# RWKV-7 / HGRN2 block on one core: the last head outputs read back through dead state tiles, masks and bounds built ahead of x, and a planner reserve of 0.8 in place of 0.45

## The chip, the cores and the metric

The kernel runs on one core of one Trainium2 chip. The metric is the device time of one execution in microseconds (us). The engines are named as the profile names them: PE is the matrix engine (PEld its weight loads), DVE the vector engine, ACT the scalar engine, POOL the GpSimd engine, SP the engine whose queue issues the DMAs. Each of them takes its instructions strictly in the order in which they were written, and waits at one whose input isn't there.

## The reference

One residual block on 512 tokens of 1024 channels, in float32:

```python
xn = rmsnorm(h, attn_pre_norm)
z = xn @ w_in                                  # 1024 -> 4096 + 3328 + 2048 columns
o_a = hgrn2_chunkwise(q, log(f), 1 - f, v)     # 8 heads of 128, chunks of 32
y = rwkv7_scan(r, w, k, v, -kk, kk * a)        # 16 heads of 64, state 64 x 64
merged = sigmoid(ga) * (o_a' @ w_branch_a) + sigmoid(gb) * (o_b @ w_branch_b)
h = h + rmsnorm(merged @ w_out, attn_post_norm)
h = h + rmsnorm(conv_ffn(rmsnorm(h, ffn_pre_norm)), ffn_post_norm)
```

`o_b` is made from `y` by a norm per head, a bonus term and the gate `g`.

## The kernel before

**Products in three passes.** Every large product is made of a high and a low part in fp32r: hi·hi, hi·lo and lo·hi. For each block of 128 columns a raw weight tile of 128x1024 is loaded from HBM (`raw`, two buffers in the pool `wraw`), ACT casts it (`whi_t`), POOL or DVE subtracts (`wlo_t`), and PE runs 24 matmuls of 128x512 into a PSUM bank (`zps`). The product that gives the HGRN values runs 256 wide (`vps`).

**Stage 0 (lines 483 to 651), written out by hand.** It loads x, multiplies the unnormalised x (`xuh`, `xul`) by the first five blocks of `w_in` and divides by the row norm afterwards (`rbs`, the results lie in the tile `ini`), so that PE needn't wait for the norm. Then it makes the normalised x (`xr`, cast to `xh`, rest in `xl`, eight pieces) that all later blocks use, and the first two weight tiles of the HGRN value product (`vn0`, `vn1`). `masks()` and `more_masks()` build the triangular masks of the chunks, `consts()` and `more_consts()` the lower bounds of the HGRN gate (`fa`, `fb`, `nfb`). In the kernel before, `more_masks()` and `more_consts()` are DVE's last work of the stage.

**Stage 1 (up to `plan.run()`), ordered by a planner.** The token mixers are written as generators that yield one instruction at a time: `lora_in`, `front`, `solve` and `chain` for RWKV (eight pairs of heads), `hgrn` for HGRN, `load`, `splits`, `gemm` and `evac` for the weights and the products. The class `Plan` gives each candidate a time at which its inputs would be ready (ends of earlier instructions by a cost table, plus a hop between engines), takes the earliest, and writes it out. `MARGIN` is added to the ready time of every PE instruction whose input or bank comes from another engine, so that it is placed later among PE's other matmuls. `AT0` gives the times at which DVE, ACT and POOL start, counted from PE. The plan is only an order: nothing on the chip waits for its times.

`chain(hb)` is the serial part: eight chunks, in each three PE steps (`us`, `yp` banks) with DVE between them. After its last chunk it makes the head norm (`ys`, `ym`, `yss`), transposes (`yt`), multiplies by the gate (`gps`) and stores to `ob_d`. The last pair of heads stays in SBUF instead.

`ob_in()`, spawned when the last chain ends, loads the other seven outputs back from `ob_d` and splits them into `oh1` and `ol1` (`oh`, `ol` in the profile). The three products `B1` with `w_branch_b` that end the stage need all eight. Before, it uses the `raw` tiles of the weights, and holds the counter `live["raw"]`, for which `load()` waits too.

**Stage 2** is the rest: the branch products (`yps`), `w_out` (`mix`), and the FFN (`zps` and `dn` by lines 354 to 356). The diff doesn't touch it.

In the trace the helper at line 237 or 387 records nearly all instructions of stages 1 and 0, so that tiles, not lines, tell them apart.

Of the kernel before, what the change touches and what calls it, by code (L numbers as in the profile page):

```python
# [16 lines left out]
P = 128  # L17
# [25 lines left out]
NWIN = 66  # L43
NX = 2
RAWS = 1
MARGIN = 0.45
AT0 = (4, 3, 1)
XG = ((0, 0),)
MORD = ((0, 0), (1, 0), (2, 0), (3, 0), (0, 1), (1, 1), (2, 1), (3, 1))
WOT = (7.0, 9.2, 13.5, 15.0)  # L50
# [28 lines left out]
class Plan:  # L79
# [76 lines left out]
    def cost(self, op):  # L156
        out = op.outs[0]
        n = out.free_size()
        scalars = sum(a.free_size() == 1 for a in op.ins) if n > 1 else 0
        far = any(a.space == PSUM for a in op.ins + op.outs)  # L160
        if op.key == "T":
            n, m = op.args[2].free_size() if op.name == "matmul" else n, op.args[1].free_size()
            if op.args[1].dtype == F32R:
                op.us = n / 2400 + (0.0165 if n > 256 else 0.013)
                if op.args[1].shape[0] < P:
                    op.us *= 1.86
            elif op.name == "transpose":
                op.us = 0.109 if n == 128 else 0.055
            elif n == 64 and m == 64:
                op.us = 0.111 if out.offset < 64 * out.ap[0][0] else 0.0535  # L170
            elif n == 64 and m == 128:
                op.us = 0.195
            elif n == 128 and op.args[1].shape[0] == 64:
                op.us = 0.118
            elif n == 32:
                op.us = 0.044 if m == 32 else 0.155
            else:
                op.us = max(0.218, n / 600)
            op.form = tuple(32 if x <= 32 else 64 if x <= 64 else P for x in (op.args[1].shape[0], m))
        elif op.key == "V":  # L180
            if op.name == "tensor_reduce":
                n = op.ins[0].free_size()
            rate = 160 if op.name == "reciprocal" else 960
            if op.name in ("tensor_copy", "tensor_scalar", "tensor_single_scalar") and not far:
                rate = 1920
            op.us = 0.069 + n / rate + 0.061 * scalars
            if op.name == "tensor_tensor_scan":
                op.us = 0.069 + n / 480
            if n == 64 and out.shape[0] == 64 and far:
                op.us += 0.07  # L190
            op.shared = not far and op.name in ("tensor_copy", "tensor_scalar", "tensor_single_scalar", "tensor_tensor",
                                                "scalar_tensor_tensor", "tensor_tensor_scan")
        elif op.key == "A":
            op.us = (0.051 if far else 0.093) + n / 1200 + (0.093 if scalars or len(op.outs) > 1 else 0.0)
            if far and n == 256 and out.shape[0] < P:
                op.us += 0.11
            elif n <= 64:
                op.us += 0.1
        elif op.key == "G":
            op.us = 0.147 + n / (470 if op.name == "tensor_tensor" else 840)  # L200
            if op.kw.get("op") == ALU.pow:
                op.us = 0.3 + n * 0.165
        else:
            op.us = 0.475
# [70 lines left out]
def block_kernel(ctx: ExitStack, tc: tile.TileContext, out: bass.AP, xT: bass.AP, xN: bass.AP,  # L275
# [22 lines left out]
    def rsq(t, n, eps, seq=lambda op: op):  # L298
        seq(G.tensor_single_scalar(t, t, eps, op=ALU.add))
        seq(G.tensor_tensor(t, t, mhalf[:, 0:n], op=ALU.pow))  # L300
# [28 lines left out]
    def split_unit(src, hi=None, lo=None, eng=None):  # L329
        raw = wraw.tile([P, 1024], F32, name="raw", tag="raw")  # L330
        nc.sync.dma_start(raw, src)
        if hi is None:
            hi, lo = ring_tiles()
        eng = eng or G
        for key, op in zip(("hi", eng), split(hi, lo, raw, eng)):
            if key in wlast:
                after(op, wlast[key])
            wlast[key] = op
        return hi, lo
# [7 lines left out]
    def seq(key, op):  # L347
        if key in last:
            after(op, last[key])
        last[key] = op  # L350
        return op
# [147 lines left out]
    with tc.tile_pool(name="init", bufs=1) as ip, tc.tile_pool(name="pinit", bufs=1, space=PSUM) as pi:  # L499
# [103 lines left out]
        for k in range(KD):  # L603
            init_mm(2, k)
            if k == KS:
                for t in range(NT):
                    Ti.matmul(sps[:, t : t + 1], acc[0][:, t * P : t * P + P], ones[:, 0:1], start=True, stop=True)
        Vi.tensor_single_scalar(ss, sps, 1.0 / D, op=ALU.mult)
        rsq(ss, NT, EPS, lambda op: seq("Gi", op))
        dg = ip.tile([P, NT, P], F32, name="dg")  # L610
        for t in range(NT):
            Ai.activation(dg[:, t], ident, AF.Identity, scale=ss[:, t : t + 1])
        init_w(B_V, V, "Vi")
        Ai.activation(le, le, AF.Exp)
        masks()
        for k in range(KD):
            init_mm(3, k)
            if k == KR:
                for t in range(NT):
                    Ti.matmul(rb[:, t * P : (t + 1) * P], ones, dg[:, t], start=True, stop=True)  # L620
        vn0 = split_unit(whi[0, 0], None, None, V)
        seq("Ai", wlast["hi"])
        seq("Vi", wlast[V])
        Ai.copy(rbs, rb)
        Ai.copy(zs0[2], zps[2])
        for k in range(KD):
# [2 lines left out]
        for k in range(KD + 1):  # L629
            if k < KD:  # L630
                xrs[k] = ip.tile([P, S], F32, name="xr", tag="xr", bufs=6)
                Vi.scalar_tensor_tensor(xrs[k], xt[:, k], pc("g_pre", k), rbs, op0=ALU.mult, op1=ALU.mult)
                Ai.copy(xh[:, k], xrs[k])
            if k >= 1:
                j = k - 1
                Vi.tensor_tensor(xl[:, j], xrs[j], xh[:, j].bitcast(F32), op=ALU.subtract)
        Vi.tensor_tensor(zs0[0], zs0[0], rbs, op=ALU.mult)
        Vi.tensor_tensor(zs0[2], zs0[2], rbs, op=ALU.mult)
        Vi.tensor_tensor(zs0[3], zps[3], rbs, op=ALU.mult)
        vn1 = (wspl.tile([P, 1024], F32R, name="whi_t", tag="hi"), wspl.tile([P, 1024], F32R, name="wlo_t", tag="lo"))  # L640
        init_wh(None, vn1, whi[0, 1])
        wturn[0] += 1
        rawf = wraw.tile([P, 1024], F32, name="raw", tag="raw")
        nc.sync.dma_start(lwr0, wlg[0, :, 0 : 2 * P])
        nc.sync.dma_start(rawf, win[B_F])
        Vi.tensor_tensor(zs0[4], zps[4], rbs, op=ALU.mult)
        Vi.tensor_tensor(zs0[1], zs0[1], rbs, op=ALU.mult)
        more_masks()
        more_consts()
        hi_pri.__exit__(None, None, None)  # L650

    cin.close()
# [350 lines left out]
    def ob_in():  # L1003
        for k in range(0, HB - 1, 2):
            n = min(2, HB - 1 - k)
            yield done(("post", k + n - 1))
            yield lambda: live["raw"] < 2
            live["raw"] += 1
            raw = wraw.tile([P, 1024], F32, name="raw", tag="raw")
            rv = raw.rearrange("p (k s) -> p k s", k=2)[:, 0:n]  # L1010
            yield D1.dma_start(rv, ob_d[k : k + n].rearrange("k p s -> p k s"))
            hi, lo = (o[:, k : k + n] for o in osb)
            yield A1.copy(hi, rv)
            yield V1.tensor_tensor(lo, rv, hi.bitcast(F32), op=ALU.subtract)
            live["raw"] -= 1
            for i in range(n):
                fin.add(("obin", k + i))

# [594 lines left out]
```

## Time and profile before

| | us |
|---|---|
| median of 3 runs | 1237.76 (1235.39 to 1238.46) |
| the profiled execution, whole | 1233.13 |
| its span in the trace | 1231.4 |
| PE busy | 1174.2 (95%) |
| DVE busy | 718.1 (58%) |
| POOL busy | 546.8 (44%) |
| ACT busy | 523.1 (42%) |

A row of the timeline gives the start, the length, the engine, the line, what is written from what, the shape, the count, and in brackets how long the engine stood idle before it and what ended that. The row of a window gives its length, and for PE, PEld, DVE, ACT and POOL the busy time and the number of instructions, then the clock that PE was granted (1.00 is full), the share of the DMA engines and GB/s. A row of waits gives the total, the number and the longest.

### The profile page before, as it was taken

The numbers are of one execution on the slowest core, as the hardware profiler recorded it, in microseconds if no ns is written. First come the engines' busy times: TensorE is split into PE (matmuls) and PEld (weight loads), VectorE is DVE, ScalarE is ACT, GpSimd is POOL, SyncE is SP. The second block draws the span as 40 slices with busy tenths as digits, with TensorE's granted clock in tenths as the row PEclk, the third lists the DMA queues.
The fourth block names the chain that finished last, engine by engine and source line by source line (L and its number), as shares of the span: only waits on it lengthen the run. The fifth ranks groups of instructions, "written<-read, shape, count | busy, mean of one in ns | idle before, by whom it ended". The sixth has DMA issues, their size and how long they took to land. (4 is left out here: it accounts for less than half of the span.)

```text
span 1231.4 us, 19053 instructions
## 1 busy us (share of the span) xinstructions
PE 1174.2 (95%) x7140; PEld 964.4 (78%) x7140; DVE 718.1 (58%) x1607; ACT 523.1 (42%) x1010; POOL 546.8 (44%) x572
## 2 busy tenths in 40 slices
PE   8789999999999999989999699999999999999997
PEld 7667778878787888767888587887988888888786
DVE  5899788797798776876673535336432323222213
ACT  6534544545464454433454333226443433433321
POOL 2154344342545243433344445423465755756521
PEclk9899999998999999999999799999999999999999
DMA  5122311212232222222323357364433322324232
GB/s 180 52 73 61 87 59 48 79 39 80 62 87 76 87 77 68 71 82 60 90 63 101 113 166 271 103 205 137 127 97 95 110 86 86 103 75 121 83 116 86
DMA packets 57244, 118.83 MB, mean 96 GB/s; under 512 B 21952, under 2 KB 25152, under 8 KB 57152
## 3 DMA queue, kind: packets, MB, share of 16 engines
q1 hardware_dynamic: 57152, 117.62, 31.2%
q8 instruction: 56, 0.92, 0.3%
q14 instruction: 36, 0.29, 0.1%
HBM read 104.22 MB, written 13.37 MB: 95 GB/s over the span
## 5 line engine op out<-in xcount | busy, mean ns | idle before, releaser
L237 POOL TENSOR_TENSOR wlo_t<-raw,whi_t 128x256 fp32r<-128x256 f32 x280 | 227.0, 840 | 298.4 <-ACT whi_t L237 283.9
L312 POOL TENSOR_TENSOR wlo_t<-raw,whi_t 128x1024 fp32r<-128x1024 f32 x75 | 182.9, 2446 | 85.9 <-ACT whi_t L312 85.8
L237 PE MATMUL zps<-xh,wlo_t 128*128 128x512 f32 x488 | 202.5, 415 | 0.0
L237 PE MATMUL zps<-xh,whi_t 128*128 128x512 f32 x488 | 201.5, 413 | 0.0
L237 PE MATMUL zps<-xl,whi_t 128*128 128x512 f32 x488 | 201.1, 412 | 0.0
L312 ACT CAST whi_t<-raw 128x1024 fp32r<-128x1024 f32 x77 | 80.1, 1048 | 159.8 <-DMA raw<-wup 65.9
L1474 DVE SCALAR_TENSOR_TENSOR u<-zps,pr,u 128x511 f32<-128x511 f32 x40 | 30.0, 750 | 187.7 <-ACT u L1473 186.9
L237 ACT CAST whi_t<-raw 128x1024 fp32r<-128x1024 f32 x74 | 77.4, 1046 | 123.8 <-PE zps L237 55.6
L354 PE MATMUL zps<-x2h,whi_t 128*128 128x512 f32 x320 | 124.7, 390 | 0.0
L356 PE MATMUL zps<-x2h,wlo_t 128*128 128x512 f32 x320 | 124.7, 390 | 0.0
L355 PE MATMUL zps<-x2l,whi_t 128*128 128x512 f32 x320 | 124.5, 389 | 0.0
L237 PEld LDWEIGHTS zps<-xh,whi_t 128*128 128x128 f32 x488 | 93.7, 192 | 17.1 <-issue 0.7
L237 PEld LDWEIGHTS zps<-xh,wlo_t 128*128 128x128 f32 x488 | 93.9, 192 | 16.7 <-issue 0.7
L237 PEld LDWEIGHTS zps<-xl,whi_t 128*128 128x128 f32 x488 | 93.5, 192 | 17.2 <-issue 0.7
L356 PEld LDWEIGHTS zps<-x2h,wlo_t 128*128 128x128 f32 x320 | 60.1, 188 | 12.7
L354 PEld LDWEIGHTS zps<-x2h,whi_t 128*128 128x128 f32 x320 | 60.1, 188 | 12.6
L355 PEld LDWEIGHTS zps<-x2l,whi_t 128*128 128x128 f32 x320 | 60.1, 188 | 12.5
L1499 POOL TENSOR_TENSOR th<-th,u 128x512 f32<-128x512 f32 x22 | 28.4, 1291 | 72.4 <-DVE u L1475 72.4
L1473 ACT ACTIVATE u<-zps,pr 128x512 f32<-128x512 f32 x40 | 31.0, 775 | 39.4 <-PE zps L356 39.4
L237 PEld LDWEIGHTS us<-sv,X 128*128 128x128 f32 x256 | 37.6, 192 | 6.9 <-DVE sv L237 2.9
L237 PEld LDWEIGHTS yp<-sv,X 128*128 128x128 f32 x256 | 37.9, 192 | 6.1 <-DVE sv L237 1.3
L355 PE MATMUL yps<-ol,whi_t 128*128 128x512 f32 x104 | 40.9, 394 | 1.7 <-DVE ol L312 1.7
(392 smaller groups left out, 2661.6 us busy)
## 6 DMA issues: line engine op xcount, KB each, us to landing
raw<-win SPq DMA_DIRECT2D x64, 512.0 KB, 3.7
raw<-wup SPq DMA_DIRECT2D x44, 512.0 KB, 3.6
raw<-wdn SPq DMA_DIRECT2D x22, 512.0 KB, 3.6
raw<-wbr SPq DMA_DIRECT2D x16, 512.0 KB, 3.9
raw<-whi SPq DMA_DIRECT2D x8, 512.0 KB, 3.7
sg_d<-sg SPq DMA_DIRECT2D x16, 256.0 KB, 2.1
gate<-sg_d SPq DMA_DIRECT2D x8, 512.0 KB, 5.6
raw<-wout SPq DMA_DIRECT2D x8, 512.0 KB, 3.5
```

The costliest lines, as they stand in the source:

```text
L237: op.ins_ = self.seq(op.key, op.fn(*op.args, **op.kw))
L312: return A.copy(hi, raw), eng.tensor_tensor(lo, raw, hi.bitcast(F32), op=ALU.subtract)
L354: T.matmul(o, lh, rh, start=start, stop=False)
L355: T.matmul(o, lh, rl, start=False, stop=False)
L356: T.matmul(o, ll, rh, start=False, stop=stop)
L1473: A.activation(u, ps, AF.Identity, scale=pc("cw2", b), bias=pc("cb", b))
L1474: V.scalar_tensor_tensor(u[:, 1:S], ps[:, 0 : S - 1], pc("cw1", b), u[:, 1:S], op0=ALU.mult, op1=ALU.add)
L1499: G.tensor_tensor(th, th, uv_, op=ALU.mult)
```

## The change

Four things: `MARGIN` from 0.45 to 0.8; `AT0` from (4, 3, 1) to (5.5, 2.5, 0.0), with one more shape (128 elements from PSUM, under 128 partitions) that is costed 0.11 dearer on ACT; stage 0 in another order; and `ob_in()` through two new tiles of the names `sv` and `bk` instead of `raw`. `sv` holds the chain's state and `bk` the front's keys; their pool has one buffer for each name, so that a new tile of the name takes the place of the old one when that is dead. Both have the size of a raw tile.

```diff
-MARGIN = 0.45
-AT0 = (4, 3, 1)
+MARGIN = 0.8
+AT0 = (5.5, 2.5, 0.0)
...
-            if far and n == 256 and out.shape[0] < P:
+            if far and n in (128, 256) and out.shape[0] < P:
...
+        Ai.activation(le, le, AF.Exp)
+        masks()
         Vi.tensor_single_scalar(ss, sps, 1.0 / D, op=ALU.mult)
+        more_consts()
+        more_masks()
         rsq(ss, NT, EPS, lambda op: seq("Gi", op))
...
         init_w(B_V, V, "Vi")
-        Ai.activation(le, le, AF.Exp)
-        masks()
...
-        vn0 = split_unit(whi[0, 0], None, None, V)
-        seq("Ai", wlast["hi"])
-        seq("Vi", wlast[V])
         Ai.copy(rbs, rb)
...
+            if k == 2:
+                vn0 = split_unit(whi[0, 0], None, None, V)
+                seq("Ai", wlast["hi"])
+                seq("Vi", wlast[V])
...
-        Vi.tensor_tensor(zs0[3], zps[3], rbs, op=ALU.mult)
         vn1 = (wspl.tile([P, 1024], F32R, name="whi_t", tag="hi"), wspl.tile([P, 1024], F32R, name="wlo_t", tag="lo"))
...
+        Vi.tensor_tensor(zs0[3], zps[3], rbs, op=ALU.mult)
         Vi.tensor_tensor(zs0[4], zps[4], rbs, op=ALU.mult)
         Vi.tensor_tensor(zs0[1], zs0[1], rbs, op=ALU.mult)
-        more_masks()
-        more_consts()
...
-            yield lambda: live["raw"] < 2
-            live["raw"] += 1
-            raw = wraw.tile([P, 1024], F32, name="raw", tag="raw")
-            rv = raw.rearrange("p (k s) -> p k s", k=2)[:, 0:n]
+            raw = mx.tile([P, NCH, 2, 64], F32, name="sv" if k % 4 else "bk")
+            rv = raw.rearrange("p (k n) h c -> p k (n h c)", k=2)[:, 0:n]
...
-            live["raw"] -= 1
```

The order of the instructions shows what these do. The first place is the end of stage 0 on DVE; in this piece of the difference, rows with a minus stood there before and rows with a plus stand there now. `ini` are the normalised first products, `wlo_t` is the low part of `vn1`, and the rows that leave are masks and bounds.

```order
+L387 TENSOR_TENSOR wlo_t<-raw,whi_t 128x1024
 L387 TENSOR_TENSOR ini<-zps_176,ini 128x512
-L387 TENSOR_TENSOR wlo_t<-raw,whi_t 128x1024
 L387 TENSOR_TENSOR ini<-zps_177,ini 128x512
 L387 TENSOR_TENSOR ini<-ini 128x512
-L387 TENSOR_TENSOR strict<-incl,ident 64x64 x2
-L387 COPY mo<-strict 128x64 x2
-L387 TENSOR_TENSOR mf<-mf,bm_146 128x64
-L387 TENSOR_TENSOR mf<-mf,strict 128x64
-L387 TENSOR_SCALAR mf<-mf 128x64
-L387 TENSOR_TENSOR lsum<-le 128x8
-L387 RECIPROCAL lsum<-lsum 128x8
```

The thirteen small instructions (four more rows of them follow) now stand right behind `ss`, before the first `xr`; the low part of `vn0` has moved the other way, from ahead of the eight `xr` to behind the third.

The second place is ACT behind the last chunk of the last chain. Before, these rows stand there; `oh` is the split of the read-back, `hf`, `p`, `hq`, `hg` belong to HGRN's last head, `lgh` to the gate:

```order
L237 CAST oh_7164<-raw 128x1024
L237 ACTIVATE ys<-ys 128x512
L237 ACTIVATE p_7191<-hf,fa,fb 128x16x16 x2
L237 CAST oh_7164<-raw 128x1024
L237 CAST lgh<-lgr 128x128
L237 CAST oh_7164<-raw 128x1024
L237 ACTIVATE hq<-zps 128x512
L237 CAST whi_t<-raw 128x1024
L237 CAST oh_7164<-raw 128x512
L237 COPY ys<-yt 64x4x64 x4
L237 ACTIVATE hg<-zps 128x512
L237 CAST whi_t<-raw 128x1024
```

And these now (`on` is HGRN's last norm, `sg` a sigmoid gate that is stored):

```order
L237 ACTIVATE ys<-ys 128x512
L237 CAST oh_7345<-bk 128x1024
L237 CAST lgh<-lgr 128x128
L237 CAST whi_t<-raw 128x1024
L237 ACTIVATE sg<-zps 128x512
L237 CAST oh_7345<-sv 128x1024
L237 ACTIVATE on,hss<-ops 128x128 x3
L237 COPY ys<-yt 64x4x64 x4
L237 CAST oh_7345<-bk 128x1024
L237 ACTIVATE on,hss<-ops 128x128
L237 CAST oh_7345<-sv 128x512
L237 CAST whi_t<-raw 128x1024
```

HGRN's last head is nearly through by now, the head norm's square stands ahead of the first `oh`, and only two `oh` stand ahead of the copies from `yt` (four before).

The third place is on PE, in the middle of stage 1, where the scores of one HGRN head (`hsc`) meet a chain and a front. So it stood before in head 2:

```order
L237 MATMUL hsc<-qi,kj 64x64
L237 MATMUL hsc<-qi,kj 32x32 x4
L237 MATMUL us<-sv,X_1840 128x64 x2
L237 MATMUL aps<-zwah,lw 128x512
L237 MATMUL aps<-zas,lw 128x512
L237 MATMUL hsc<-qi,kj 32x32 x2
L237 MATMUL yp<-sv,X_1840 128x64 x2
L237 MATMUL hsc<-qi,kj 64x64
```

And now, in a later head:

```order
L237 MATMUL us<-sv,X_4374 128x64 x2
L237 MATMUL hsc<-qi,kj 32x32 x5
L237 MATMUL hsc<-qi,kj 64x64
L237 MATMUL hsc<-qi,kj 32x32 x6
L237 MATMUL hsc<-qi,kj 64x64
L237 MATMUL hsc<-qi,kj 32x32
L237 MATMUL nps<-blk_102,sq 128x2
L237 MATMUL yp<-zs,qd_517 128x64
```

In both, no 512-wide matmul of a weight block (`zps`) stands between the small ones. Before, the 28 small groups of a head's scores stand so, with rows of a chain and a front among them, in one head; now in three, in one of them with rows of `solve` and a single `zps` row as well.

## The prediction

> **What bounds the kernel now.** I read the page first, then windows over the three stages, then PE's waits and what ended them.
>
> ```profile
> span 1231.4 us, 19053 instructions
> PE 1174.2 (95%) x7140; PEld 964.4 (78%) x7140; DVE 718.1 (58%) x1607; ACT 523.1 (42%) x1010; POOL 546.8 (44%) x572
> PEclk9899999998999999999999799999999999999999
> 100.00:650.00 550.00, 530.47 (x4070) 434.31 (x4069) 433.58 (x1162) 263.25 (x614) 229.68 (x314) 0.99 0.24 71
> 640.34 0.40 PE L237 MATMUL zps<-xl,whi_t 128*128 128x512 f32 x1
> 640.57 0.40 PE L237 MATMUL zps<-xh,wlo_t 128*128 128x512 f32 x1
> ```
>
> PE is busy for 1174.2 of 1231.4 us, and it is the bound in every stage; its busy time is made of a fixed list of matmuls, of which the wide ones follow each other every 0.23 us (640.34 to 640.57). The change takes no matmul away. It can only win what PE loses: 57.2 us of idle time, and stretches in which the granted clock is below full (the 7 and the 8s of PEclk). The middle, 100 to 650, holds 19.5 us of the idle time; the rest sits in few places, and the change is aimed at two of them.
>
> **The start.** Stage 0 ends in a wait.
>
> ```profile
> 28.60 1.23 DVE L312 TENSOR_TENSOR wlo_t<-raw,whi_t 128x1024 fp32r<-128x1024 f32 x1 [3.75 <-ACT whi_t L312]
> 33.34 1.41 DVE L387 SCALAR_TENSOR_TENSOR xr<-xt,pr,ini 128x512 f32<-128x512 f32 x2
> 46.82 0.39 PE L237 MATMUL vps<-wlo_t,xh 128*128 128x256 f32 x1 [1.32 <-DVE wlo_t L387]
> 47.88 0.45 DVE L387 TENSOR_TENSOR strict<-incl,ident 64x64 f32<-64x64 f32 x2
> 50.10 0.17 DVE L387 TENSOR_SCALAR nfb<-fb 128x8 f32<-128x8 f32 x1
> 50.19 0.72 ACT L237 ACTIVATE zwa<-ini,cm 128x512 f32<-128x512 f32 x1 [6.13 <-DVE fb L387]
> 53.08 0.60 ACT L237 CAST zwah<-zwa 128x512 fp32r<-128x512 f32 x1
> 53.79 0.55 PE L237 MATMUL wps<-zwah,lw 64*128 64x512 f32 x1 [4.79 <-ACT zwah L237]
> 52.00:56.00 4.00, 2.01 (x5) 1.35 (x6) 2.54 (x4) 3.91 (x7) 1.18 (x2) 0.75 0.00 0
> 56.00:60.00 4.00, 4.00 (x18) 3.34 (x16) 3.64 (x6) 3.49 (x6) 0.90 (x1) 0.50 0.02 4
> ```
>
> PE waits 1.32 for the low part of `vn1`, then 4.79 for `zwah`; `zwah` waits for `zwa`, and `zwa` stood 6.13 behind DVE's last bounds. The masks and bounds (47.88 to 50.27) take 2.4 us of DVE there. Now they stand behind `ss`, in the 3.75 us in which DVE waits for ACT ahead of 28.60, so they cost nothing while they fit: 2.4 into 3.75, and their masks are copied by ACT while it would wait for the norm. If they don't, the whole x preparation slips by the excess. With ACT's copies and the `vn0` split out of the way, the first `xr` can follow the split that ends at 29.83, say at 29.9 where it was 33.34: 3.4 earlier, less the 1.2 of the `vn0` split that now stands inside: 2.2. `zwa` comes 2.2 + 2.4 = 4.6 earlier, of which I keep 4.1; a weight cast that the planner now puts ahead of `zwah` takes about 1 back. So `zwah` is ready at about 50.6 instead of 53.7. PE, without the 1.32, would be at `wps` at 47.7, and the new order puts 15 half-width matmuls more ahead of it, 15 times half of 0.23, or 1.7: 49.4. What is late next is `zwah` by 1.1 us. The two waits shrink from 6.1 to 1.1: **−5.0**. Bounds: −6.1 if `zwa` needs only its own input, −3 if it still hangs on the last `ini`.
>
> Behind the wait the clock was 0.75 for 2.01 busy us and 0.50 for 4.00: 0.5 + 2.0 = 2.5 us lost. With an idle time of 1.1 this goes: **−2.5** (0 if a short wait drops it too).
>
> **The front of the first head.**
>
> ```profile
> 76.16 0.37 PE L237 MATMUL scb<-X,bk 64*128 64x128 f32 x1 [1.22 <-DVE bk L237]
> 82.57 0.46 PE L237 MATMUL sc<-X,bk 64*128 64x128 f32 x2 [2.74 <-DVE X L237]
> 93.44 0.66 PE L237 MATMUL tp<-ident,bk 128*128 128x128 f32 x4 [1.21 <-DVE bo L237]
> ```
>
> 5.2 us, all behind DVE. The new order has 66 wide matmuls instead of 49 between `nps` and `sc`, but DVE now has the eight reciprocals ahead of `bk`, and between `bps` and `tp` the 16 wide matmuls have become the scores and one wide one. The second wait goes, the third grows: **−1** (−4 to +2).
>
> **The end of stage 1.** This is the largest single place.
>
> ```profile
> 668.01 0.55 PE L237 MATMUL yp<-sv,X 128*128 128x64 f32 x4
> 669.16 0.69 DVE L237 TENSOR_TENSOR ys<-ys 128x512 f32<-128x512 f32 x1 [1.80 <-ACT ys L237]
> 676.57 1.67 POOL L237 TENSOR_TENSOR yss<-yss,mhalf 128x8 f32<-128x8 f32 x1
> 681.00 10.26 SPq L237 DMA_DIRECT2D raw<-ob_d  x2
> 684.40 1.04 ACT L237 CAST oh<-raw 128x1024 fp32r<-128x1024 f32 x1 [4.49 <-DMA raw<-ob_d]
> 685.97 0.69 DVE L237 SCALAR_TENSOR_TENSOR hq<-hq,zps 128x512 f32<-128x512 f32 x1 [3.54 <-ACT hq L237]
> 687.41 1.09 PE L237 MATMUL yt<-ident,ys 128*128 128x128 f32 x4 [8.10 <-DVE ys L237]
> 693.67 0.62 ACT L237 CAST oh<-raw 128x512 fp32r<-128x512 f32 x1 [6.80 <-DMA raw<-ob_d]
> 695.74 0.80 PE L237 MATMUL gps<-zgzh,lgh 128*128 128x512 f32 x1 [2.65 <-ACT ys L237]
> 680.00:700.00 20.00, 9.94 (x28) 7.77 (x29) 10.96 (x15) 6.45 (x11) 7.91 (x9) 0.66 0.30 96
> raw<-ob_d SPq DMA_DIRECT2D x3, 512.0 KB, 3.6
> 746.04 0.50 PE L355 MATMUL yps<-ol,whi_t 128*128 128x512 f32 x1 [1.69 <-DVE ol L312]
> ```
>
> The read-back needs `raw` buffers that the weights hold, so its DMAs stand in SP's queue (10.26 us for two), ACT stands at `oh`, DVE at `hq` behind ACT, and the norm that PE's `yt` needs stands behind `hq` although POOL had its part at 678.2. PE idles 8.10 and then 2.65, and its clock is 0.66 over these 20 us: 9.94 busy us lose 9.94 × 0.34 = 3.4.
>
> Now `bk` is dead since the last front and `sv` at the last chain matmul, so the first two DMAs issue behind `lgr` at once, and the weight loads no longer queue with them. I count from the last `yp`. The norm: from `ys` at 669.16 on, six steps of about 0.7 on DVE and ACT bring it to 4.4 by my estimate, and POOL's two (the second 1.67) to 7.3. DVE's own queue: the first read-back issues at about 0.9, lands 3.6 later, cast 1.04, subtraction 1.2 (a split of that size at 28.60), two small HGRN steps, then the scaled `ys` 0.7: about 8.6. PE's rows up to `yt` are now 29 wide matmuls and ten small HGRN ones, 39 × 0.23 = 9.0 (before, 47 wide ones, 10.8; the trace has 687.41 less 8.10 less 668.56, 10.7). So the wait goes, with 0.4 to spare, and what is late next is again the read-back: each us that a load needs beyond 4 is a us at `yt`. `gps` stands 14 wide matmuls, 3.2 us, behind `yt`, and the copies between them no longer wait for two read-backs: no wait. I keep 0.4 of risk: **−10.3** and **−3.4** for the clock. Bound: a load that shares the engines takes 5.5 rather than 3.6, which gives 1.5 back, and no clock is lost. The reuse makes ACT and DVE free `bk` before the third load: behind it in SP's queue stands a weight for `B1`, which starts some 20 us after the chain; that is the cover. HGRN's last head now ends ahead of `B1` instead of inside it, so the 1.69 at 746.04 goes as well: **−1.7**.
>
> **The middle, where the reserve works.**
>
> ```profile
> PE fps L237 <- DVE Tn L237: 5.4, 6, 2.2
> PE dps L237 <- DVE Tn L237: 4.4, 4, 1.5
> PE yt L237 <- DVE ys L237: 3.9, 4, 2.0
> ```
>
> These and five smaller groups, all on DVE too, make up the 19.5 us of idle time between 100 and 650, in some 20 waits of about 1 us. `MARGIN` places each waiting step 0.35 us, or one and a half wide matmuls, later per hop, and behind two hops 0.7. Taking 0.35 off each of 20 waits gives 7, taking 0.7 off gives 12 or so, since the small ones end at zero: **−7** (−14 to +2, because a faster PE also leaves DVE, busy for 433.6 of 550, less time). The price of the reserve is latency: between two steps of a chain stand seven wide matmuls, before six. It shows nowhere while such matmuls are left, and 69 still stand behind the last chain (before 129).
>
> The clock is the other side.
>
> ```profile
> 287.67 0.76 PE L237 MATMUL us<-sv,X 128*128 128x64 f32 x4 [0.30 <-DVE sv L237]
> 294.21 0.80 PE L237 MATMUL zps<-xh,wlo_t 128*128 128x512 f32 x1
> 292.00:296.00 4.00, 4.00 (x28) 3.47 (x27) 3.52 (x19) 2.44 (x6) 0.00 (x0) 0.62 0.00 0
> 296.00:300.00 4.00, 4.00 (x13) 3.38 (x13) 2.33 (x7) 1.63 (x3) 1.13 (x2) 0.53 0.00 0
> 540.00:548.00 8.00, 7.61 (x75) 6.13 (x76) 1.59 (x11) 2.04 (x4) 0.92 (x2) 0.79 0.35 82
> 560.00:568.00 8.00, 6.84 (x87) 6.16 (x87) 2.70 (x7) 3.26 (x9) 1.38 (x5) 0.79 0.23 68
> ```
>
> At 292 to 300 the clock falls to about 0.6 although PE waited at most 0.30: ahead of 294.21 stand some 7 us of small matmuls only, scores among chain steps. It costs 4 × 0.38 + 4 × 0.47 = 3.4 us. At 540 and 560 it costs 7.61 × 0.21 + 6.84 × 0.21 = 3.0 more, behind waits. In the new order three heads have such a bunch, by my estimate 4 to 6 us long. Three falls would cost 10.2, two 6.8; I take 8.4, against 6.4 now: **+2** (−6 to +8).
>
> A rule bears on this. The Trainium skill, "TensorE: Matmul & The Clock Gate", Part 1, says that PE falls to half clock after an idle window of about 3.4 us and needs about as long a busy one to come back. The fall behind 4.79 us agrees; that at 292 does not, and the measurement decides.
>
> **The sum.** −5.0 − 2.5 − 1 − 10.3 − 3.4 − 1.7 − 7 + 2 = −28.9. The profiled execution took 1233.13 (span and 1.7 around it), so its like would take 1204.2. It was faster than the three timed runs; against their median, 1237.8 − 28.9 = **1208.9**.
>
> **The rivals.**
>
> The middle gives nothing: DVE's lag grows with PE's speed, the 19.5 us stay, and three to four bunches cost the clock, +4 instead of +2. −28.9 + 7 + 2 gives 1218 (to 1222 with a fourth). For it speaks that every wait quoted there ends at DVE, which the change makes no faster.
>
> The bunches cost nothing: only waits of several us drop the clock. Then the middle's term is −6.4 instead of +2: 1200.5. Against it speaks 292 to 300. It is what the rule of the Trainium skill named above would make of the new order.
>
> The read-back is late again, behind `lgr` and a `sg` store in SP's queue, so that ACT stands at `oh` as before and the end gives nothing: −28.9 + 13.7 gives 1222.6. Against it: the loads now come before the weights.
>
> It is slower: the longer chain. One wide matmul more in each of 24 steps is 24 × 0.23 = 5.5 us a head, 44 us over eight. This is free as long as matmuls are left behind the last chain; 69 × 0.23 = 16 us are. Should DVE's lag push the chains by more than that, PE would idle through the rest: 44 − 28.9 gives 1253. It decides from the point at which the wait ahead of `B1` passes 29 us.
>
> The change doesn't do what it says: fitted to the planner's own times, it moves the waits to other hops, and only part of the start's 5 us stays: about 1234 to 1239, no difference. That is within 0.3% (3.7 us), about what a measurement of this kernel can tell.
>
> **How the numbers follow.** Forecast 55%, middle nothing 18%, bunches free 9%, read-back late 7%, no difference 5%, slower 6%. The forecast's own range, from the terms' bounds taken together and not all at one end, is 1200 to 1217. To 1198 below and 1226 above lie the forecast and the next three, with some of each lost at the ends: about 8 in 10. Faster than 0.3%: 0.55 + 0.18 + 0.09 + 0.07 = 0.89; same 0.05; slower 0.06.
>
> **What would show it.** Right: `zwa` at about 46 and no wait over 1.5 us at `wps`; clock 1.0 at 56 to 60; `yt` of the last head without a wait, `oh` waiting under 1.5 us, SP's read-backs under 2 us each; PE's waits on `fps`, `dps` and `yt` in the middle halved; two or three falls of the clock behind bunched scores. Wrong: a new wait of several us at `yps` or `B1`, waits in the middle of 19.5 us or more, or falls of the clock in more than four places.

## The result and the profile after

| | before | after |
|---|---|---|
| median, us | 1236.58 (4 runs, 1234.72 to 1238.46) | 1197.4 (4 runs, 1196.47 to 1199.69) |
| profiled execution, us | 1233.13 | 1197.6 |
| its span, us | 1231.4 | 1195.9 |
| PE idle in the span, us | 57.2 | 25.1 |

The ratio is 0.9686, 95% interval 0.9664 to 0.9708: clearly faster, by 39.2 us between the medians and by 35.5 between the profiled executions. Forecast were 28.9 less and 1208.9 us; the time lies 2.6 us under the forecast's own range (1200 to 1217) and 0.6 under the wide one (1198 to 1226).

First the page of the changed kernel.

```profile
span 1195.9 us, 19056 instructions
PE 1170.8 (98%) x7140; PEld 961.8 (80%) x7140; DVE 722.5 (60%) x1607; ACT 523.2 (44%) x1010; POOL 544.7 (46%) x572
PEclk9999999999999999999999999999999999999999
```

PE does the same 7140 matmuls, now in 98% of the span, and none of the forty slices has a clock under nine tenths. Where the time went shows in its windows (columns as before: length, busy time of PE and of the others, then the clock).

```profile
52.00:56.00 4.00, 3.91 (x22) 3.15 (x23) 3.51 (x7) 3.97 (x7) 0.00 (x0) 1.00 0.33 121
56.00:60.00 4.00, 3.92 (x22) 3.09 (x21) 2.19 (x7) 3.97 (x7) 3.26 (x4) 1.00 0.00 0
100.00:650.00 550.00, 542.57 (x4125) 444.52 (x4126) 438.72 (x1182) 269.54 (x627) 232.97 (x323) 0.99 0.26 75
660.00:680.00 20.00, 19.63 (x101) 16.00 (x101) 15.09 (x24) 13.04 (x28) 13.64 (x15) 1.00 0.47 155
```

The two windows behind the start, 0.75 and 0.50 before, have their full clock. The middle idles 7.4 us (550 less 542.57) where it idled 19.5. The 20 us in which the last head's `yt` and `gps` stand idle 0.4 at full clock; before, these two stood in 680 to 700, which idled 10.1 at 0.66.

The start, by the timeline:

```profile
25.63 0.46 DVE L387 TENSOR_TENSOR strict<-incl,ident 64x64 f32<-64x64 f32 x2
28.48 1.23 DVE L312 TENSOR_TENSOR wlo_t<-raw,whi_t 128x1024 fp32r<-128x1024 f32 x1 [1.43 <-ACT whi_t L312]
29.67 1.42 DVE L387 SCALAR_TENSOR_TENSOR xr<-xt,pr,ini 128x512 f32<-128x512 f32 x2
34.10 1.23 DVE L312 TENSOR_TENSOR wlo_t<-raw,whi_t 128x1024 fp32r<-128x1024 f32 x1 [1.64 <-ACT whi_t L312]
43.75 0.73 ACT L237 ACTIVATE zwa<-ini,cm 128x512 f32<-128x512 f32 x1 [0.50 <-DVE ini L387]
48.35 0.63 ACT L237 ACTIVATE zwa<-zwa 64x512 f32<-64x512 f32 x1 [2.01 <-DVE zwa L237]
50.13 0.60 ACT L237 CAST zwah<-zwa 128x512 fp32r<-128x512 f32 x1
50.83 0.47 PE L237 MATMUL wps<-zwah,lw 64*128 64x512 f32 x1 [1.43 <-POOL wlo_t L237]
52.09 0.47 PE L237 MATMUL wps<-zws,lw 128*128 128x512 f32 x1 [0.37 <-ACT zws L237]
```

The masks run inside DVE's wait for ACT: that wait has shrunk from 3.75 to 1.43, and the split behind it starts at 28.48 (28.60 before). The first `xr` follows at 29.67. The low part of `vn0` (34.10) brings a wait of 1.64 for ACT, so that DVE's last `xl` ends only 0.8 earlier than before. `zwa` starts at 43.75 instead of 50.19, but its second step (48.35) waits 2.01 for DVE, which has the last splits and `ini` ahead of it; `zwah` starts at 50.13 instead of 53.08. The wait at `wps` is 1.43. The row names POOL's `wlo_t`, which ends at the same time; what `wps` reads is `zwah`, and that ends at 50.73, 0.1 ahead of the matmul, so I put the wait down to `zwah`.

The front of the first head, in PE's timeline:

```profile
75.91 0.37 PE L237 MATMUL scb<-X,bk 64*128 64x128 f32 x1 [0.77 <-DVE bk L237]
80.22 0.46 PE L237 MATMUL sc<-X,bk 64*128 64x128 f32 x2 [0.63 <-DVE X L237]
90.13 0.66 PE L237 MATMUL tp<-ident,bk 128*128 128x128 f32 x4 [0.24 <-DVE bo L237]
```

5.2 us of waits have become 1.6; the third, which I expected to grow, is the smallest.

The end of stage 1, and the first branch product behind it. First two more rows of SP's queue before (the prediction shows that of 681.00):

```profile
668.49 6.89 SPq L237 DMA_DIRECT2D raw<-ob_d  x2
690.93 0.33 SPq L237 DMA_DIRECT2D raw<-ob_d  x1
```

And the changed kernel:

```profile
661.99 0.55 PE L237 MATMUL yp<-sv,X 128*128 128x64 f32 x4
663.53 0.40 SPq L237 DMA_DIRECT2D bk<-ob_d  x1
663.98 0.46 SPq L237 DMA_DIRECT2D sv<-ob_d  x1
667.54 1.05 ACT L237 CAST oh<-bk 128x1024 fp32r<-128x1024 f32 x1 [0.51 <-DMA bk<-ob_d]
668.17 1.67 POOL L237 TENSOR_TENSOR yss<-yss,mhalf 128x8 f32<-128x8 f32 x1
670.69 0.38 SPq L237 DMA_DIRECT2D bk<-ob_d  x1
671.07 1.21 DVE L237 TENSOR_TENSOR ys<-ys,yss 128x512 f32<-128x512 f32 x1
671.17 0.45 SPq L237 DMA_DIRECT2D raw<-wbr  x1
672.34 0.66 PE L237 MATMUL yt<-ident,ys 128*128 128x128 f32 x4
673.98 0.33 SPq L237 DMA_DIRECT2D sv<-ob_d  x1
674.74 1.05 ACT L237 CAST oh<-bk 128x1024 fp32r<-128x1024 f32 x1 [0.20 <-DMA bk<-ob_d]
710.50 0.50 PE L355 MATMUL yps<-ol,whi_t 128*128 128x512 f32 x1 [0.98 <-DVE ol L312]
```

A single issue of a read-back takes 0.33 to 0.46 in SP's queue, before as now; the 6.89 and 10.26 of the rows of before reach from one issue to the end of the next. What has changed is when the four come: counted from the end of the last `yp`, at −0.1, 6.4, 12.4 and 22.4 us before, and now at 1.0, 1.4, 8.2 and 11.4. ACT waits 0.51, 0, 0.20 and 0.54 at the four `oh` (0.47, 3.15, 4.49 and 6.80 before), and `yt` and `gps` have no wait. The cover at `yt`, the work that PE has until its input comes, is just enough: the scaled `ys` ends at 672.28, `yt` starts at 672.34. Of 1.69 at `yps` 0.98 is left.

What is left of the waits in the middle, in PE's waits from 100 to 650 (total, times, longest):

```profile
PE fps L237 <- DVE Tn L237: 2.9, 2, 1.5
PE yt L237 <- DVE ys L237: 1.4, 2, 1.1
PE yp L237 <- DVE zs L237: 1.0, 2, 0.8
```

**The clock, cell by cell.** Narrow windows laid over each trace show that a fall goes to exactly half clock and lasts 3.4 us or a whole multiple of it, and that the falls of one execution lie on one grid of 3.41 us. I call a stretch of that grid a cell, and count fallen cells. The kernel before has ten between 30 us and the end of the FFN; the changed kernel has three, at 123, 509 and 823 us. Here is the one at 509, with a cell on each side.

```profile
505.47:508.88 3.41, 3.41 (x58) 2.94 (x46) 2.57 (x10) 2.75 (x7) 0.00 (x0) 1.00 0.00 0
508.88:512.29 3.41, 3.41 (x21) 2.94 (x21) 2.61 (x12) 1.34 (x4) 0.00 (x0) 0.50 0.53 84
512.29:515.71 3.42, 3.42 (x20) 2.88 (x20) 1.67 (x6) 2.91 (x7) 1.74 (x3) 1.00 0.30 115
594.22:597.63 3.41, 3.41 (x65) 2.95 (x66) 1.56 (x4) 0.86 (x3) 0.00 (x0) 1.00 0.02 5
```

The first row is a cell inside a bunch of scores without a `zps` row (505.0 to 509.3 by the timeline), PE busy all through; the next cell has 0.50. The bunch at 592.4 to 597.4 is longer, its cell (last row) has as many small matmuls, and no fall follows. Of the six bunches of 4 to 6 us in this kernel (stretches of stage 1 without a matmul 256 or 512 wide of a weight block) one dropped the clock.

### The profile page after: what moved, and what is told of

The parts are those of the page before. It is cut to its first block, busy times and chain, and to the rows that moved or that the text cites. A ratio compares the mean times of both kernels' runs of the same rounds, so it can differ in the third digit from the quotient of the medians.

```text
span 1195.9 us, 19056 instructions
## 1 busy us (share of the span) xinstructions
PE 1170.8 (98%) x7140; PEld 961.8 (80%) x7140; DVE 722.5 (60%) x1607; ACT 523.2 (44%) x1010; POOL 544.7 (46%) x572
## 5 line engine op out<-in xcount | busy, mean ns | idle before, releaser
L237 PE MATMUL zps<-xl,whi_t 128*128 128x512 f32 x488 | 198.4, 407 | 0.0
L237 ACT COPY ys<-us 64x128 f32<-64x128 f32 x64 | 16.7, 261 | 62.4 <-DVE sv L237 47.1
```

The lines of the kernel that those rows point to most:

```text
L237: op.ins_ = self.seq(op.key, op.fn(*op.args, **op.kw))
```

## The experiments

Theory A, after the result: the terms of the prediction are the right places, each worth what the waits and the clock of its place show. Its rivals: the worth of a part hangs on the others (the reserve above all), and what the clock loses isn't set by how long a bunch is. All times are medians, all ratios are to the kernel before on the same chip. PE idle and fallen cells come from one profiled execution each.

**The parts alone, on the kernel before.** The read-back:

```diff
-            raw = wraw.tile([P, 1024], F32, name="raw", tag="raw")
+            raw = mx.tile([P, NCH, 2, 64], F32, name="sv" if k % 4 else "bk")
```

> The kernel before with the read-back through the dead tiles and nothing else. Theory A (each place pays by itself): the wait of 8.1 us at the last head's transpose, the 2.65 us behind it and the 3.4 us of lost clock go, 14 us in all, 1222 to 1224. Theory B (the planner's reserve does nearly all, the tiles matter little): under 4 us, 1233 or more. Theory C (the wait only moves, since with the old reserve four splits of the read-back still stand ahead of the copies on ACT): 4 to 8 us, with a new wait of 3 us or more at the transpose or at the gate product.

1221.8 us, ratio 0.9887 (0.9838 to 0.9936): 14 us less than the 1235.9 there, the size of the two terms for the end of stage 1 (10.3 and 3.4). In its timeline:

```profile
684.30 0.63 PE L237 MATMUL yt<-ident,ys 128*128 128x128 f32 x4 [0.86 <-DVE ys L237]
```

8.10 us of wait have become 0.86, there is no wait at `gps`, and no cell falls between 650 and 800. The end's mechanism is shown.

The reserve:

```diff
-MARGIN = 0.45
+MARGIN = 0.8
```

> The kernel before with the reserve at 0.8 and nothing else. Theory A: the middle's waits fall from 19 to about 8 us and those of the first head's front by 2 to 3, while the end keeps its wait of some 10 us: 12 to 18 us faster, 1219 to 1225. Theory B: 30 us or more faster, under 1207. Rival D (the longer chains cost what the reserve saves): within 5 us of before.

1235.53 us, ratio 0.9988 (0.9968 to 1.0007): no difference. The windows and the timeline of this kernel say why.

```profile
100.00:650.00 550.00, 533.72 (x4033) 440.02 (x4032) 430.15 (x1148) 258.66 (x603) 224.88 (x314) 0.97 0.24 70
194.75:198.16 3.41, 1.37 (x11) 1.14 (x9) 3.38 (x4) 0.24 (x1) 3.29 (x7) 1.00 0.02 5
198.16:201.57 3.41, 1.70 (x8) 1.68 (x8) 3.07 (x5) 0.54 (x2) 1.39 (x2) 0.50 0.28 85
```

```profile
709.75 0.79 PE L237 MATMUL gps<-zgzh,lgh 128*128 128x512 f32 x1 [8.28 <-ACT ys L237]
```

The middle idles 16.3 us instead of 19.5, but its clock is 0.97: ten cells fall there, four before. One new wait of 3.8 us at a `vp`, which begins in the first of these two cells, is followed by four fallen cells in a row. The last `yp` slides from 668 to 688, and the wait at the end, which was 8.10 at `yt`, is now 8.28 at `gps`. Over the span PE idles 50.6 us (57.2 before), and half of its busy time in fallen cells is 21.7 (14.3): the one gain eats the other.

Stage 0 (the lines of the change's diff for stage 0, nothing else):

```diff
+        masks()
+        more_consts()
+        more_masks()
...
+            if k == 2:
+                vn0 = split_unit(whi[0, 0], None, None, V)
```

> The kernel before with only stage 0 in its new order. Theory A: the waits of 6.3 us at the first gate products shrink to 1 or 2 and the 2.5 us of lost clock behind them go: 6 to 8 us faster, 1229 to 1231. Theory B: under 2 us. Rival E (the order of stage 1 was made for the old start, so that PE reaches the same matmul 1.7 us earlier): wait of 3 us or more left, 3 to 5 us faster.

1234.88 us, ratio 0.9996 (0.9968 to 1.0023): no difference that ten runs show (1226.9 to 1240.43). The wait at `wps` shrinks to 2.25 and `B1` comes 3.6 earlier in the profiled execution, but a cell still falls behind `wps`, and eleven fall in all (ten before).

The start times, with the cost line that goes with them:

```diff
-AT0 = (4, 3, 1)
+AT0 = (5.5, 2.5, 0.0)
```

> The kernel before with only the planner's start times (and the one dearer shape on ACT). Theory A: the start's wait stays at 5 to 6 us, the rest is another order of the same quality: within 4 us of before. Theory B (the start times are what the first heads lack): the first 60 us of stage 1 win 5 us or more.

1227.35 us, ratio 0.9922 (0.9896 to 0.9947): 8.6 less than the 1235.9 of that chip. This was no term of mine. Windows and timeline:

```profile
100.00:650.00 550.00, 537.63 (x4109) 441.66 (x4108) 443.73 (x1190) 267.68 (x630) 224.78 (x314) 0.98 0.24 71
```

```profile
670.92 0.80 PE L237 MATMUL zps<-xh,whi_t 128*128 128x512 f32 x1 [5.76 <-ACT whi_t L237]
```

The middle idles 12.4 instead of 19.5, the last `yp` comes at 648, 20 us earlier; part of that is given back behind the chain, above all at a weight that is cast only when its load has landed (ACT waits 4.33 for it, behind the last read-backs, and PE 5.76): the read-back through `raw` now holds up the weights.

**One part undone, on the changed kernel.** The edits are those above, the other way round.

> The changed kernel with the reserve back at 0.45. Theory A (the places add): it gives back the middle, 12 to 18 us: 1209 to 1215. Theory B (the reserve does nearly all): 1225 or more. Rival D (the reserve costs as much as it saves): within 5 us of the changed kernel, under 1203.

1212.17 us, ratio 0.9804 (0.9781 to 0.9828): 14.8 more than the changed kernel. The middle idles 13.3 (7.4), 650 to 800 idles 7.5 (1.4), six cells fall (three).

> The changed kernel with the read-back through raw tiles again. Theory A: the waits of about 10 us and the lost clock of 3 come back at the last head's transpose: 1209 to 1213. Theory B: under 1201, since HGRN's last head now stands ahead of the read-back on ACT. If the longer chains leave only 69 wide matmuls as cover, more than 14 us, over 1212.

1204.47 us, ratio 0.9743 (0.9723 to 0.9764): 7.1 more, not 14. HGRN's last head is nearly through by then in this order, so that less stands behind the late read-backs. The long wait is in PE's timeline at

```profile
688.74 0.63 PE L237 MATMUL otp<-ident,on 128*128 128x128 f32 x4 [3.66 <-DVE on L237]
```

> The changed kernel with stage 0 in its old order. Theory A: 5 to 8 us slower, 1203 to 1206, the wait for the first gate products at 3 to 5 us again. Theory B: within 2 us.

1204.03 us, ratio 0.9729 (0.9699 to 0.976): 6.6 more. The waits of 1.32 and 3.72 are back, and two fallen cells with them: 3.9 us of idle time more between 30 and 100 us, and half of PE's busy time in the two cells is 2.5.

So the parts don't add: undone one by one from the change, reserve, read-back and stage 0 cost 28.5 together; done alone, they give some 15.

**The reserve's size, and what it works with.** On the changed kernel:

```diff
-MARGIN = 0.8
+MARGIN = 1.2
```

> The changed kernel with the reserve at 1.2. If the middle's waits are what the reserve buys, only 7.5 us of them are left at 0.8: it can win 3 to 5 us more, 1192 to 1195, as long as matmuls are left behind the last chain. Rival D (latency): the chains get longer by another 5 us a head, the cover behind the last one runs out, and it is slower than the changed kernel by 5 us or more.

1256.43 us, ratio 1.0162 (1.0137 to 1.0187): slower than before. The timeline is that of my rival with the longer chain:

```profile
729.66 1.12 PE L237 MATMUL yp<-sv,X 128*128 128x64 f32 x4 [0.37 <-DVE sv L237]
740.77 1.09 PE L237 MATMUL yt<-ident,ys 128*128 128x128 f32 x4 [9.99 <-DVE ys L237]
741.51 0.78 PE L237 MATMUL zps<-oh,whi_t 128*128 128x512 f32 x1
```

The last `yp` comes 68 us later than at 0.8, all other wide matmuls are used up, so 10 us of wait stand open at `yt` and `B1` follows at once; 14 cells in a row fall from 696 on.

Then the values between, and the reserve with one other part on the kernel before.

> The changed kernel with MARGIN 0.65. Theory P (the reserve's worth goes smoothly from 1212.2 at 0.45 to 1197.4 at 0.8): 1200 to 1207, waits between 100 and 650 us of 8 to 11 us, the last yp at about 650. Theory Q (each setting is a schedule of its own, and what counts is the number of clock falls of 3.4 us and of late waits that it happens to have): anything from 1194 to 1215, the number of falls in the profile explaining 1.7 us each.

1210.87 us, ratio 0.9798 (0.9762 to 0.9833): as at 0.45, so the worth isn't smooth. The middle idles 11.7 us, nine cells fall.

> The changed kernel with MARGIN 0.95. By the slide of the last yp (662 at 0.8, 730 at 1.2, 17 us per 0.1) the last yp lies at about 688 and its yt has no cover left: a wait of 5 to 12 us there, and 1206 to 1222. Rival: the read-back's own last reads still cover it and the waits inside fall further below 7.4: 1192 to 1197, better than 0.8.

1223.09 us, ratio 0.9897 (0.9862 to 0.9933). The last `yp` stands at 694, `yt` behind it waits 9.99, `B1` follows at once, and seven cells in a row fall from 687: the cover is gone already here. No setting tried beats 0.8.

> The kernel before with the new AT0 (and the planner's cost line) and MARGIN 0.8; the read-back goes through raw and stage 0 has its old order. Theory A (the reserve pays only together with the new start times, the other two parts then add what undoing them took away): the changed kernel's 1197.4 plus 6.6 (stage 0) plus 7.1 (read-back) is some 1211, 16 less than AT0 alone (1227.4). Theory B (the reserve pays because the read-back has moved): about AT0's 1227, or more, with a wait of some 8 us for the read-back ahead of the last gate. Between 1207 and 1216 is A, over 1222 is B, between them both have a share.

1211.12 us, ratio 0.9799 (0.9757 to 0.9841): A. Its window:

```profile
100.00:650.00 550.00, 542.16 (x4132) 444.05 (x4131) 439.61 (x1176) 269.93 (x627) 234.90 (x326) 1.00 0.25 75
```

> The kernel before with the new read-back (dead state tiles) and MARGIN 0.8; AT0 (4, 3, 1) and the old stage 0. Theory A (the reserve pays only with the new start times): as the read-back alone, 1221.8, within 4, since with the old start times the last head's yp slid to 688 when the reserve was raised alone and the gate's work stood behind it; the yp to yt distance has no cover any more. Theory B (the reserve pays with the read-back): 1221.8 less some 14, so about 1207.

1226.31 us, ratio 0.9916 (0.9887 to 0.9944): 4.5 more than the read-back alone: half a us outside A's end and far from B's. With the old start times nine cells fall in the middle (six with the read-back alone).

What the middle (100 to 650) does under the two tables of the planner:

| | idle us | fallen cells |
|---|---|---|
| before | 19.5 | 4 |
| reserve alone | 16.3 | 10 |
| start times alone | 12.4 | 5 |
| both | 7.8 | 1 |
| the whole change | 7.4 | 2 |

Idle times nearly add (−3.2, −7.1, both −11.7). Fallen cells don't, and they are what makes the reserve worth nothing alone. Behind the new start times the reserve is worth 16 us (1227.35 to 1211.12): 4.6 of idle time and four cells here, and at the end, 650 to 800, where the start times alone idle 15.7, another 10.1 and two cells.

**What drops the clock.** Eight bursts of 32x32 matmuls whose results aren't used, ahead of eight blocks of the FFN, where wide matmuls run without a wait; 26 to 132 calls, rising, and in a second kernel falling. The trace has two matmuls for each call.

```diff
+    BURST = {4: 26, 6: 39, 8: 53, 10: 66, 12: 79, 14: 92, 16: 105, 18: 132}
     for j in range(NF):
+        for _ in range(BURST.get(j, 0)):
+            T.matmul(dmy[0:32, 0, 0:32], ident[0:32, 0:32], ident[0:32, 0:32], start=True, stop=True)
```

> The changed kernel with eight bursts of 32x32 matmuls into an unused bank, added between the blocks of the FFN, by estimate 2, 3, 4, 5, 6, 7, 8 and 10 us long in this order. Theory F (a stretch of small matmuls drops the clock like a wait, but only if it fills the window in which the activity is counted): no fall behind 2 and 3 us, a fall behind every one from 7 us on, in between by chance. Theory G (only idle time drops it, as the page on the clock gate reads): no fall behind any. Theory H (any bunch of 4 us drops it, as the prediction had it): falls from 4 us on, six in all. Time: 45 us of bursts and 1.7 to 3.4 us for each fall.

> The same eight bursts, the longest first. Theory F: the same answer at 2, 3, 7, 8 and 10 us, and another one at some length between 4 and 6, since the window runs by itself. Theory G: no fall. Theory H: the same six falls.

1246.95 and 1247.45 us, one timed execution each. Length of each burst in us (some lengthened by the fall itself), and the cells that fell:

| calls | 26 | 39 | 53 | 66 | 79 | 92 | 105 | 132 |
|---|---|---|---|---|---|---|---|---|
| rising | 1.83, 0 | 2.65, 1 | 3.54, 0 | 4.36, 0 | 5.80, 2 | 6.01, 1 | 8.07, 2 | 10.82, 3 |
| falling | 1.83, 0 | 2.65, 0 | 3.54, 0 | 4.36, 1 | 5.41, 1 | 6.27, 1 | 7.91, 2 | 11.27, 3 |

No burst holds an idle PE, so idle time alone as the cause is out. In each run a fall follows five of the eight bursts (six sizes over both runs). From 5.4 us on the clock always falls, below that by chance: 2.65 did once, 3.54 never. That fits a cell of the free grid that a burst must fill, wholly or nearly.

What is it that a cell must have too little of? I worked out, from the timeline's records, the columns streamed in each cell, each matmul weighted by the share of the 128 rows that it uses, against wide ones that follow every 0.227 us (1.0). A matmul that lies in two cells is shared out between them by time. In 17 executions (all here but the last run below), from 30 us to the end of the FFN, 83 cells at full clock have less than 0.27 by this measure, and behind 81 of them the clock falls; the other 15 falls come from cells between 0.27 and 0.41, where 141 others have none. No fall comes from a cell above that. In the changed kernel the cell ahead of 508.88 has 0.23, that ahead of 123.18 (1.5 us of waits at `fps`) 0.23, that ahead of 822.9 (2.0 us of wait) 0.25; the cells inside the other bunches have 0.31 or more. 19 of the 96 falls, ten of them behind the bursts, follow a cell with less than 0.3 us of idle time. This was fitted after the fact, so it needs a run of its own: the same bursts with 128 rows, and with 128 outputs. (The shares in the expectations are lower, 0.09 and 0.38: they are on a scale 6% lower and take 35 ns a matmul; by the trace the bursts run at 32 ns at full clock and 53 at half.)

```diff
-            T.matmul(dmy[0:32, 0, 0:32], ident[0:32, 0:32], ident[0:32, 0:32], start=True, stop=True)
+            T.matmul(dmy[0:32, 0, 0:32], ident[:, 0:32], ident[:, 0:32], start=True, stop=True)
```

> The changed kernel with the eight bursts of the run with rising bursts (26 to 132 instructions, 1.83 to 10.82 us there), whose matmuls now use 128 rows of the array instead of 32 (128x32 weights, 32 columns moved, 32 outputs); their results are not used. In the run with bursts of 32 rows every fall of the clock lasted 3.4 us or a multiple of it, the falls of one run lie on one grid of 3.41 us, and the cell of the grid ahead of a fall has few rows times columns streamed: below some 0.25 of what fits into it; bursts of 32 rows and 32 columns every 35 ns reach 0.09. Theory I (rows times columns streamed in a cell of the grid decide): these bursts reach 32 columns x 128 rows every 35 ns, 0.38, if their pace stays: no fall behind any burst, of whatever length, and none up to 10 us; if the pace were below 51 ns per instruction still 0.26. Theory C (columns alone): 0.38 in both, so falls behind the bursts as before: all from 5.4 us on. Theory S (few outputs, or short instructions): falls as before, 5 to 6 of 8 bursts. Theory O (idle time only) is already out: the bursts hold no idle time and the clock fell to 0.50 behind six of eight.

1235.71 us, 11.2 less than with 32 rows, one execution each and on two chips; inside the profiles PE's busy time is 9.8 us less, with six fallen cells fewer. First the rising bursts with 32 rows by their cells, then those with 128:

```profile
1067.26:1070.67 3.41, 3.41 (x114) 3.41 (x111) 0.00 (x0) 1.12 (x2) 3.41 (x3) 1.00 0.02 5
1070.67:1074.09 3.42, 3.42 (x62) 3.35 (x60) 0.00 (x0) 0.00 (x0) 2.56 (x2) 0.50 0.72 244
1074.09:1077.50 3.41, 3.41 (x9) 2.64 (x9) 0.00 (x0) 0.00 (x0) 0.00 (x0) 0.50 0.17 67
```

```profile
1097.68:1101.09 3.41, 3.41 (x114) 3.41 (x111) 0.00 (x0) 1.22 (x2) 3.41 (x3) 1.00 0.02 5
1101.09:1104.51 3.42, 3.42 (x114) 3.42 (x112) 0.00 (x0) 0.00 (x0) 2.67 (x2) 1.00 0.68 234
1104.51:1107.92 3.41, 3.41 (x24) 2.83 (x22) 0.00 (x0) 1.05 (x1) 2.28 (x1) 1.00 0.20 78
```

The same number of matmuls in a cell, just as busy, 32 columns each: with 32 rows (a share of 0.11) the next two cells run at half clock, with 128 rows (0.45) nothing falls, behind any of the eight bursts, up to 8.54 us. Theory I holds. Columns alone, short instructions and outputs alone are out, since all three are the same in both runs. So is the area (rows times outputs) with one limit: by it the bursts of 128 rows have 0.11 and no fall, while 56 of the 96 falls come from cells above 0.12.

```diff
-            T.matmul(dmy[0:32, 0, 0:32], ident[0:32, 0:32], ident[0:32, 0:32], start=True, stop=True)
+            T.matmul(dmy[:, 0, 0:32], ident[0:32, :], ident[0:32, 0:32], start=True, stop=True)
```

> The same bursts with 32 rows as at first, but 128 outputs (32x128 weights, 32 columns moved). Theory I (rows times columns): 0.09 of the array's streaming, falls behind every burst from 5.4 us on, as with 32 rows and 32 outputs: 5 to 6 of 8 bursts, each 3.4 us or a multiple. Theory M (outputs times columns decide): 0.38, no fall. Theory A (rows times outputs, the area in use): 0.09, falls too; the run with 128 rows and 32 outputs, at the same area, tells A from I: A has falls there, I none. If both runs show falls it is the area or the short instructions, if neither does, rows and outputs both count.

1438.39 us, clock 0.916, falls of 2 to 16 cells behind every burst. It tells less than it should: these bursts run at 112 ns a matmul at full clock (213 at half) instead of 32, so that the share is 0.03 by rows and 0.13 by outputs, both far below 0.27. Falls are what either would give.

## Why the prediction was wrong, point by point

The places were right and nothing was given back, but the time came out 11.5 us under the forecast. 6.6 of it lie in the sum, profile to profile (28.9 against 35.5), and the steps that failed there are the two terms of the middle. The other 4.8 lie in the sum's last step, which took 28.9 off the median: the median of the kernel before lies 4.6 above its profiled execution, that of the changed kernel 0.2 below. In the 39 timed executions of the kernel before that the experiments' results list, the time goes with the mean granted clock (correlation −0.76): the fastest four, 1231.4 to 1231.9 us, had 0.984, the five with 0.977 or less took 1236.6 to 1242.2. The profiled one had 0.985, so it lost less to the clock than most; the four of the changed kernel all had 0.994 to 0.996.

In the terms' two kinds: idle time −25.0 forecast and −32.1 measured; clock −3.9 forecast, and by half of PE's busy time in the fallen cells (14.3 before, 5.1 after) −9.2 measured. That makes 41.3; 5.8 stand against it as PE busy time that I can't place. (Half is too much for small matmuls: those of the bursts come every 53 ns at half clock and every 32 at full. How much of the 5.8 that is, no run shows.) Over all fourteen schedules the account holds: span less idle less that half is 1159 to 1166 us in each, while the span runs from 1196 to 1255.

- **The start** (−5.0 and −2.5): waits 6.1 to 1.8, −4.3, and the clock is full. The masks fit into the 3.75 and the first `xr` stands at 29.67 (29.9), as forecast. Behind that two steps were off and made up for each other: the x preparation ends 0.8 earlier, not 2.2, and `zwa` starts 6.4 earlier, not 4.1, but then stands behind DVE for its second step, so that `zwah` comes 2.9 earlier (3.1 forecast). That the wait at `wps` came out at 1.43 (1.1) is in part luck. Undone the part costs 6.6 of the 7.5.
- **The first front** (−1): −3.5. The growth of the third wait didn't come.
- **The end of stage 1** (−10.3, −3.4): the waits and the clock loss went whole, and the read-back alone gave 14. The working was less good than the result: the scaled `ys` was ready 9.7 us behind the last `yp`, not 8.6, and PE did not have to wait only because it took 9.8 to get there where I had 9.0, with a wait of 0.35 at `ops` inside. That no wait was left is in part luck. Inside the whole change the part is worth 7, since in the new order less stands behind a late read-back.
- **The `yps` wait** (−1.7): −0.7.
- **The middle's waits** (−7): −12.1, the step that failed. "`MARGIN` places each waiting step 0.35 us … later per hop" put all of it on the reserve. The start times, which I costed only at the stage's beginning, take 7.1 of the idle time out of the middle on their own; the reserve takes 3.2 alone and 4.6 behind them.
- **The middle's clock** (+2): −3.4 (four fallen cells with 6.8 of half busy time became two with 3.4), the other step that failed. I took a bunch of 4 to 6 us for a fall. The clock falls if a cell of the grid inside it streams less than about 0.27 of a wide stream; of six such bunches one did. The rival of the free bunches had the better time (1200.5) for a wrong reason: one of them did cost a fall, with PE busy all through.

The rival of the longer chain is real: it decides from 0.95 on, and gives 1256 at 1.2. The rival "the middle gives nothing" describes the reserve alone (1235.53 us), not the whole change.

The Trainium skill, "TensorE: Matmul & The Clock Gate", Part 1, has the clock judged in free-running windows of 3413 ns and switched between full and half. Every trace here agrees, with falls of 0.50 and multiples of 3.4 us. It speaks of idle windows; here cells in which PE never idled dropped the clock (0.50 behind 505.47 to 508.88), and the measurement decides.

**Still open.** Which records of the new start times remove which wait in the middle wasn't separated, nor which of its two edits (`AT0` and the cost line). And the grid lies elsewhere in each execution, so that a cell's fall in one profile needn't be there in the next: the counts of fallen cells are those of one execution each. That the kernel before spreads more (1231 to 1242 us on the other chips, ten cells) than the changed one (1196 to 1200, three) fits this, and so does the clock that goes with its times; no run moved the grid.

## What to carry to other kernels

Cost a planner's change by two sums over the whole stage, PE's idle time and its fallen clock cells, and cost every table that the planner reads: the start times did more than the reserve that the change speaks of. A reserve ahead of dependent steps pays until the chain outlasts the independent matmuls; watch the last chain step's time, since beyond that each wait stands open. Between wide matmuls, keep stretches of small ones, with the waits in them, short (bursts of 1.83 us did no harm here), or give them full 128 rows.

## What the runs showed of the hardware that I had not expected

- The clock doesn't ask whether PE is busy. Bursts of 32x32x32 matmuls, 32 ns apart with no idle time, dropped it to 0.50 always from 5.4 us on; the same bursts with 128 rows never did, up to 8.54 us.
- A fall is 3.41 us or a multiple, on one grid per execution. With 32 rows six cells more fell in the run than with 128, and PE's busy time was 9.8 us longer: 1.6 per cell.
- 32x32 weights with 128 outputs instead of 32 slowed such matmuls from 32 to 112 ns each at full clock (from 53 to 213 at half), while 128x32 weights kept the 32 ns: the pace goes with the outputs, not the rows. Why, no run here shows.
